# A fourth channel tile of the depthwise convolution on VectorE instead of TensorE

## The chip, the cores and the metric

The kernel runs on one core of a Trainium2 chip. The metric is the device time of one execution in microseconds. Five engines work side by side, each through its own fixed list of instructions: TensorE (PE; its weight loads are PEld), VectorE (DVE), ScalarE (ACT), GpSimd (POOL) and SyncE (SP). They wait for one another through semaphores. DMAs are issued from the queues of SP, POOL and ScalarE.

## The reference

One step of a two-layer streaming encoder, in float32, for two groups of requests: a prompt of 1024 frames and 8 running streams of 16 new frames each, 1152 rows in all, of width 1024. Layer 0 is differential attention beside a gated MLP. Layer 1, where the change lies, is a Conformer convolution module:

```python
xn = _rmsnorm(x, norm_g)
z = jnp.einsum('btd,de->bte', xn, w_in)
a, b, g = jnp.split(z, [C_WIDTH, 2 * C_WIDTH], axis=-1)
u = a * jax.nn.sigmoid(b)
...
c = lax.conv_general_dilated(ctx, w_dw[:, None, :], window_strides=(1,), padding='VALID',
                             feature_group_count=C_WIDTH) + b_dw
c = jax.nn.silu(_layernorm(c, ln_g, ln_b)) * jax.nn.silu(g)
y = x + jnp.einsum('btc,cd->btd', c, w_out)
```

`ctx` is `u` with 30 rows ahead of it: zeros for the prompt, the stored state for a running stream. The convolution is depthwise: each of the 1024 channels has its own 31 taps along time.

## The kernel before

Channels lie on partitions, 128 to a tile, so layer 1 has eight channel tiles, numbered 0 to 7. Each dense product is made of three float32r products (high by high, high by low, low by high; `mm3`, L157), whose weights are loaded, split into a high part on ScalarE (L145) and a low part on VectorE (L146). Weights are made one tile ahead.

`phase_conv` loops over the eight channel tiles and calls `conv_tile` (L1095) for each. It projects the 1152 rows in three chunks of 384 columns, first `b`, then `a`: six psum chunks of 24 products, from a pool `mm` of three psum buffers. ScalarE takes the sigmoid (L1133), VectorE multiplies `a` by it. Then there are two ways to do the 31 taps, and the constant `TAPS` says which tiles go the first way:

- Taps on VectorE. The product is written to a tile `u` (L1138), with the states put in by ScalarE (L1110) and the new frames by POOL (L1150). `taps()` multiplies `u`, shifted by k, with the k-th weight per channel and adds it to `cT`: for each k one instruction for the 8 streams (128 columns) and one for the prompt (1024 columns), L1171 for k = 0 and L1173 for the others. So a tile has 62 such instructions, and each depends on the one before it of the same width.
- Toeplitz products on TensorE. The product is written to `U` in another order (L1141), stored to DRAM (`s_u`, L1181) and loaded again as `X` (L1183), so that 8 time phases of a channel lie on neighbouring partitions. POOL builds the banded 32x32 weights `tw` (L1189). There are two steps, each of 80 products of 32x32x176 (`py`, L1198), which the trace lists as 160. ScalarE copies the result out (L1202), it goes through DRAM (`s_c`, L1208 to L1212) and VectorE adds the bias on the way back into `cT` (`back`, L1217 and L1220).

A tile's two Toeplitz steps are put into TensorE's list while the next tile is projected (`TOEP = (3, 4)`: behind the fourth and the fifth of its six chunks). For tile 7 they stand behind the first and second chunk of gate tile 1.

`back(i)` makes tile `i`'s taps, or its way back, and adds `cT[i]` to `msum` (L950, L952). It is called two tiles later: for a tile in `TAPS` after tile `i + 2` has been written down, for another inside tile `i + 2`. For tiles 6 and 7 it is called behind gate tiles 0 and 1. The order in which the program is written down gives each instruction a priority; a planner simulates the engines and fixes each engine's list by that.

After the eight tiles come eight gate tiles: three chunks each, from the same psum pool, with a silu on ScalarE (L980) into `sg`. Gate tiles 0 and 1 write into tiles that are also named `u`, and there are two buffers of that name for taps and gates together:

```python
u = self.up.tile([P, PAD + T + NB * 46], F32, name="u", bufs=2)
...
sg = [cp.tile([P, PAD + T + NB * 46], F32, name="u", bufs=2) for _ in range(2)]
```

The gates from 2 on (`sg`) lie in a pool that is opened where the convolution's work pool `ub` was, and so behind the last use of that, tile 7's way back. While the gate tiles are projected, the layernorm over channels runs in three column blocks (`norm_sum`, `norm_var`, `norm_apply`, L1005 to L1046), beginning behind the eleventh gate chunk. Last comes the output product, row tile by row tile.

Of the kernel before, what the change touches and what calls it, by code (L numbers as in the profile page):

```python
# [90 lines left out]
WL = ((0, 0, 2, 2), (2, 0, 2, 0))  # L91
VMID = False
TOEP = (3, 4)
TAPS = (0, 2, 4)
BACK = 3
HPT = 400
TAIL = 1
# [7 lines left out]
class Builder:  # L105
# [809 lines left out]
    def phase_conv(self):  # L915
        nc, tc, a = self.nc, self.tc, self.a
        with ExitStack() as st:
# [28 lines left out]
            def back(i):  # L946
                tiles[i][2]()
                done.append(cT[i])
                if len(done) == 2:
                    nc.vector.tensor_tensor(msum, done[0], done[1], ALU.add)  # L950
                elif len(done) > 2 and i < 7:
                    nc.vector.tensor_tensor(msum, msum, cT[i], ALU.add)  # L952

            def hooks_of(i):
                hooks = {}
                if i > 0:
                    hooks[TAIL] = [tiles[i - 1][0]]
                    for p, f in zip(TOEP, tiles[i - 1][1]):
                        hooks.setdefault(p, []).append(f)
                return hooks  # L960

            for i in range(8):
                wb = self.split_w(wp, [a["w_in1"][:, i * P:(i + 1) * P],
                                       a["w_in1"][:, D + i * P:D + (i + 1) * P]], 256)
                late = (lambda j=i - 2: back(j)) if i > 1 and i - 2 not in TAPS else None
                tiles.append(self.conv_tile(i, wb, pm, ub, cT[i], chan, wdw, (s_u, s_c), same, hooks_of(i), late))
                if i - 2 in TAPS:
                    back(i - 2)
# [126 lines left out]
    def conv_tile(self, i, wb, pm, ub, cv, chan, wdw, scr, same, hooks, late):  # L1095
# [8 lines left out]
        for n in range(2):  # L1104
            nc.tensor.transpose(ps[:, n * 120:(n + 1) * 120], sn[:120, n, :], self.ident[:120, :120])
        if i in TAPS:
            u = self.up.tile([P, PAD + T + NB * 46], F32, name="u", bufs=2)
# [20 lines left out]
        for c in range(3):  # L1128
# [7 lines left out]
            n = 384 if c < 2 else 256  # L1136
            if i in TAPS:
                mu = nc.vector.tensor_tensor(u[:, PAD + c * 384:PAD + c * 384 + n], pa_[:, :n], sb[:, :n], ALU.mult)  # L1138
# [7 lines left out]
            if c == 2:  # L1146
                nc.vector.tensor_tensor(utmp, pa_[:, 224:384], sb[:, 224:], ALU.mult)
                nw = utmp[:, 32:]
                if i in TAPS:
                    nc.gpsimd.tensor_copy(us[:, :, PAD:], nw.rearrange("p (b k) -> p b k", k=NQ))  # L1150
# [23 lines left out]

        if i in TAPS:
            return tail, (), taps
# [73 lines left out]
```

## Time and profile before

| | |
|---|---|
| median of 3 runs | 1223.09 us (1223.04 to 1224.46) |
| the profiled execution | 1223.68 us, span of its instructions 1221.9 us |
| granted TensorE clock, mean | 0.979 |
| TensorE busy | 1156.0 us |
| VectorE busy | 731.6 us |
| ScalarE busy | 456.8 us |
| POOL busy | 340.7 us |
| taps on VectorE (L1173) | 180 instructions, 779.4 to 959.4 us |
| Toeplitz products (L1198) | 1600 products in 10 steps, 829.5 to 1018.6 us |

All times inside an execution are in microseconds from the first instruction. A row of a timeline has start, duration, engine, line, operation, what is written and read, the shape, how many instructions are drawn together, and in brackets the idle time of the engine before it and what ended it. A row of a stage view has the stretch, its length, and for each engine the busy time and the number of instructions; then the granted clock, the busy share of the DMA engines, and GB/s.

### The profile page before, as it was taken

How to read it: one execution, taken by the hardware profiler on the slowest of the kernel's cores; microseconds unless marked ns; L12 is line 12 of the kernel's file. 1: busy time of each engine (PE TensorE's matmuls, PEld its weight loads, DVE VectorE, ACT ScalarE, POOL GpSimd, SP SyncE). 2: the span in 40 equal slices, each digit the busy share in tenths (PEclk: the TensorE clock that was granted, in tenths of full speed). 3: DMA queues.
4: the chain of work that ended last, by engine and by line, in shares of the span. 5: the costliest groups of instructions: out<-in, count | busy, mean ns of one | idle time of the engine just before them, and what ended most of it. 6: DMA issues, size and time to landing. Idle time of an engine off the chain costs nothing. (4 is left out here: it accounts for less than half of the span.)

```text
span 1221.9 us, 20908 instructions
## 1 busy us (share of the span) xinstructions
PE 1156.0 (95%) x7886; PEld 1024.1 (84%) x7886; DVE 731.6 (60%) x1560; ACT 456.8 (37%) x1065; POOL 340.7 (28%) x510
## 2 busy tenths in 40 slices
PE   6999999999989998679999999999999999998997
PEld 4878998899989997457777677899999899996886
DVE  4420225678788878766556444698999711377443
ACT  4431223445454545555444334312121222365221
POOL 2233223334434435413322231212131220350000
PEclk9999999999989998879999999999999999998999
DMA  8453435324132313867767635333332442113331
GB/s 302 110 169 91 144 118 172 107 71 121 46 89 78 108 50 105 301 214 242 258 226 255 192 125 190 92 91 96 93 96 90 140 134 84 35 35 104 104 104 69
DMA packets 125365, 160.33 MB, mean 131 GB/s; under 512 B 16514, under 2 KB 87194, under 8 KB 125257
## 3 DMA queue, kind: packets, MB, share of 16 engines
q1 hardware_dynamic: 109344, 106.95, 28.5%
q0 software_dynamic: 15776, 51.79, 12.9%
q8 instruction: 62, 1.02, 0.3%
q14 instruction: 39, 0.31, 0.1%
q10 hardware_dynamic: 144, 0.26, 0.1%
HBM read 119.41 MB, written 40.00 MB: 130 GB/s over the span
## 5 line engine op out<-in xcount | busy, mean ns | idle before, releaser
L157 PE MATMUL mm<-yh,wh 128*128 128x384 f32 x576 | 196.5, 341 | 3.3 <-ACT sb L1133 2.5
L157 PE MATMUL mm<-yl,wh 128*128 128x384 f32 x576 | 193.9, 337 | 0.5 <-issue 0.5
L157 PE MATMUL mm<-yh,wl 128*128 128x384 f32 x576 | 193.8, 338 | 0.3 <-DVE wl L146 0.2
L157 PE MATMUL mm<-wh,xh 128*128 128x384 f32 (+1 forms) x504 | 185.4, 369 | 2.5 <-DVE sg L468 1.4
L157 PE MATMUL mm<-wl,xh 128*128 128x384 f32 (+1 forms) x504 | 184.5, 366 | 0.9 <-DVE wl L146 0.9
L157 PE MATMUL mm<-wh,xl 128*128 128x384 f32 (+1 forms) x504 | 183.7, 364 | 0.0
L146 DVE TENSOR_TENSOR wl<-raw,wh 128x1024 fp32r<-128x1024 f32 (+1 forms) x72 | 84.3, 1178 | 104.7 <-ACT wh L145 102.7
L1173 DVE SCALAR_TENSOR_TENSOR cT<-u,cc,cT 128x128 f32<-128x128 f32 (+1 forms) x180 | 141.3, 843 | 1.0
L157 PEld LDWEIGHTS mm<-yh,wh 128*128 128x128 f32 x576 | 108.7, 189 | 6.2 <-issue 2.8
L157 PEld LDWEIGHTS mm<-yh,wl 128*128 128x128 f32 x576 | 108.6, 189 | 2.0 <-DVE wl L146 0.9
L157 PEld LDWEIGHTS mm<-yl,wh 128*128 128x128 f32 x576 | 108.7, 189 | 1.1 <-issue 0.7
L157 PEld LDWEIGHTS mm<-wh,xh 128*128 128x128 f32 x504 | 95.7, 190 | 13.3 <-DVE sg L468 1.4
L157 PEld LDWEIGHTS mm<-wl,xh 128*128 128x128 f32 x504 | 95.9, 190 | 10.5 <-DVE wl L146 1.8
L157 PEld LDWEIGHTS mm<-wh,xl 128*128 128x128 f32 x504 | 95.7, 190 | 8.7 <-DVE xl L170 0.3
L145 ACT CAST wh<-raw 128x1024 fp32r<-128x1024 f32 (+1 forms) x72 | 71.8, 1001 | 73.0 <-PE mm L157 30.9
L126 POOL TENSOR_TENSOR rr<-pw,mhalf 128x1 f32<-128x1 f32 x59 | 33.0, 559 | 200.3 <-DVE pw L125 190.8
L559 ACT ACTIVATE e<-S,nm 128x512 f32<-128x512 f32 (+5 forms) x96 | 55.1, 579 | 42.1 <-DVE nm L554 26.4
L157 PE MATMUL out<-wh,ch 128*128 128x512 f32 x144 | 59.9, 416 | 2.0 <-DVE xr L845 1.2
L157 PE MATMUL mm<-wh,ch 128*128 128x512 f32 x144 | 57.1, 397 | 4.5 <-ACT ch L1079 4.5
L551 DVE TENSOR_REDUCE nm<-S 128x1 f32<-128x512 f32 (+5 forms) x96 | 52.5, 551 | 12.6 <-PE S L546 11.9
L777 DVE TENSOR_TENSOR vl<-vraw,vh 128x1024 fp32r<-128x1024 f32 x32 | 43.2, 1351 | 26.8 <-ACT vh L776 26.6
L157 PE MATMUL out<-wh,cl 128*128 128x512 f32 x144 | 58.8, 408 | 0.0
(282 smaller groups left out, 2300.6 us busy)
## 6 DMA issues: line engine op xcount, KB each, us to landing
raw<-in_cache_k SPq DMA_DIRECT2D x32, 512.0 KB, 4.4
vraw<-in_cache_v POOLq DMA_DIRECT2D x32, 512.0 KB, 5.7
raw<-in_w_in SPq DMA_DIRECT2D x24, 512.0 KB, 5.3
raw<-in_w_out SPq DMA_DIRECT2D x16, 512.0 KB, 5.0
raw<-in_w_in SPq DMA_DIRECT2D x32, 256.0 KB, 4.0
raw<-in_w_in SPq DMA_DIRECT2D x48, 128.0 KB, 2.8
s_y<-xr POOLq DMA_DIRECT2D x9, 512.0 KB, 4.7
x<-s_y SPq DMA_DIRECT2D x9, 512.0 KB, 4.3
```

The source lines that it names most:

```text
L126: m = nc.gpsimd.tensor_tensor(out, v[:, :w], self.mhalf[:, :w], ALU.pow)
L145: nc.scalar.copy(h[:, :ks * n], raw[:, :ks * n])
L146: (low or nc.vector).tensor_tensor(l[:, :ks * n], raw[:, :ks * n], h[:, :ks * n].bitcast(F32), ALU.subtract)
L157: m = self.nc.tensor.matmul(out, lhsT=x, rhs=y, start=(i == 0), stop=(i == n - 1))
L551: nc.vector.tensor_reduce(nm[:, j:j + 1], s[:, :n], AX.X, ALU.max, negate=True)
L559: nc.scalar.activation(e[:, j * n:(j + 1) * n], S[j][:, :n], AF.Exp, bias=nv, accum_out=zz[:, j:j + 1])
L777: (nc.vector if i in VDVE else nc.gpsimd).tensor_tensor(vl, vr, vh.bitcast(F32), ALU.subtract)
L1173: nc.vector.scalar_tensor_tensor(dst, src, w1, dst, ALU.mult, ALU.add)
```

## The change

Channel tile 5 goes from the Toeplitz products to the taps; tiles 1, 3, 6 and 7 stay Toeplitz products. Nothing else is edited; what `conv_tile` and `back` do with tile 5 follows from the constant.

```diff
 VMID = False
 TOEP = (3, 4)
-TAPS = (0, 2, 4)
+TAPS = (0, 2, 4, 5)
 BACK = 3
 HPT = 400
```

## The prediction

> **What bounds the kernel now.** I read the busy shares and the chain first, then the conv layer by stage, then single engines' timelines.
>
> ```profile
> PE 1156.0 (95%) x7886; PEld 1024.1 (84%) x7886; DVE 731.6 (60%) x1560; ACT 456.8 (37%) x1065; POOL 340.7 (28%) x510
> ...
> PE 18%; DVE 1%; issue 1%; DMA 0%; ACT 0%; POOL 0%; DVEq 0%; POOLq 0%
> PE mm L157 16%; PE py L1198 1%; DMA big<-s_u 0%; DVE wl L146 0%; DVE cT L1044 0%; DVE cT L1064 0%; POOL nm L126 0%; PE ln L1009 0%; PE ln L1041 0%; PE ln L1010 0%; PE ln L1028 0%; PE ln L1029 0%; ACT wh L145 0%; DVE yo L195 0%; ACT yo L189 0%
> ```
>
> TensorE is busy 95% of the span and is nearly the whole of the last chain. The Toeplitz products (py, L1198) stand in that chain by themselves: what leaves TensorE shortens it, as long as no other engine becomes late. The stage view tells whether one does:
>
> ```profile
> core 0: us, PE busy (x) PEld busy (x) DVE busy (x) ACT busy (x) POOL busy (x), PEclk, DMA share, GB/s
> 871.00:902.00 31.00, 31.00 (x469) 29.31 (x468) 30.47 (x41) 5.96 (x17) 9.61 (x8) 1.00 0.38 110
> ...
> 927.00:959.00 32.00, 31.27 (x468) 29.19 (x467) 31.61 (x31) 5.92 (x17) 9.30 (x10) 1.00 0.36 110
> 959.00:992.00 33.00, 31.40 (x470) 29.71 (x469) 12.02 (x15) 6.30 (x17) 7.74 (x9) 1.00 0.42 125
> 1024.00:1109.00 85.00, 84.38 (x483) 81.35 (x481) 44.66 (x85) 39.25 (x74) 29.35 (x21) 1.00 0.17 54
> ...
> 961.00:1017.00 56.00, 53.88 (x793) 50.79 (x800) 14.60 (x19) 10.85 (x27) 11.59 (x14) 1.00 0.41 132
> ```
>
> The rows at 871, 927 and 959 are channel tiles 4, 6 and 7. While tile 6 is projected VectorE is full (31.61 of 32 us: the taps of tile 4); from 961 to 1017 it works only 14.60 of 56 us. The change puts a tile's taps into these 41.4 idle us.
>
> **What it takes off TensorE.** ScalarE's sigmoid of a tile's first chunk marks the pace of the tiles:
>
> ```profile
> 905.45 0.49 ACT L1133 ACTIVATE sb<-mm 128x384 f32<-128x384 f32 x1 [3.25 <-PE mm L157]
> 930.90 0.49 ACT L1133 ACTIVATE sb<-mm 128x384 f32<-128x384 f32 x1 [3.27 <-PE mm L157]
> 963.24 0.49 ACT L1133 ACTIVATE sb<-mm 128x384 f32<-128x384 f32 x1 [3.24 <-PE mm L157]
> 995.86 0.49 ACT L980 ACTIVATE u<-mm 128x384 f32<-128x384 f32 x1 [1.98 <-PE mm L157]
> ```
> ```profile
> 945.75 2.71 PE L1198 MATMUL py<-big,tw 32*32 32x176 f32 x160
> 950.67 2.62 PE L1198 MATMUL py<-big,tw 32*32 32x176 f32 x148
> 953.95 0.52 PE L1198 MATMUL py<-big,tw 32*32 32x176 f32 x12 [0.65 <-issue]
> ...
> 977.53 2.71 PE L1198 MATMUL py<-big,tw 32*32 32x176 f32 x160 [1.60 <-DMA big<-s_u]
> ```
>
> The rows are the first chunks of tiles 5, 6, 7 and of the gate. Tile 5, with no Toeplitz step inside, takes 930.90 - 905.45 = 25.45 us (six chunks of 4.24); tile 6, with both steps of tile 5 inside, 963.24 - 930.90 = 32.34 us. The difference, 6.9 us, is what tile 5's two steps cost: 2.71 and 3.28 us of products (with the 0.65 pause), and about 0.9 us around them. These 6.9 us come off. The Trainium skill, TensorEngine Tiling (Array Packing), Key Properties, says that a change of tiling mode drains TensorE; counting products alone the sum would be 6.0, and the 0.9 us more in the tile's pace agree with it.
>
> The next Toeplitz step, tile 6's first at 977.53, already waits 1.60 us for its input. That input begins with the multiplication of tile 6's last chunk on VectorE and goes through two DMAs on POOL's queue:
>
> ```profile
> 963.14 0.66 DVE L1141 TENSOR_TENSOR big<-mm,sb 128x256 f32<-128x256 f32 x1
> ...
> 965.66 0.59 POOL L1181 DMA_DIRECT2D s_u<-big  x1 [0.30 <-POOL big L1152]
> 972.34 0.92 POOL L1183 DMA_DIRECT2D big<-s_u  x1 [6.09 <-issue]
> ```
>
> From 963.14 to 977.53 are 14.4 us; TensorE has four chunks, 17.0 us, between the end of tile 6 and that step, so the multiplication may come 2.6 us after TensorE's end of the tile; now it comes 4.1 after (963.24 - 4.24 = 959.0). VectorE will now be full there. The wait lies between 0 (the DMAs meet no other traffic) and about 4 (6.6 us after); I take 3.3 for tile 6 and nothing for tile 7, so 1.7 more than now. TensorE's own balance: 6.9 - 1.7 = 5.2 us sooner.
>
> **What it puts on VectorE.**
>
> ```profile
> 805.00 7.36 DVE L1173 SCALAR_TENSOR_TENSOR cT<-u,cc,cT 128x1024 f32<-128x1024 f32 x10
> 947.81 12.88 DVE L1173 SCALAR_TENSOR_TENSOR cT<-u,cc,cT 128x1024 f32<-128x1024 f32 x8
> 960.73 1.36 DVE L952 TENSOR_TENSOR msum<-msum,cT 128x1152 f32<-128x1152 f32 x1
> 968.21 1.18 DVE L1217 TENSOR_SCALAR cT<-big,cc 128x1024 f32<-128x1024 f32 x1
> 969.32 0.45 DVE L1220 TENSOR_SCALAR cT<-big,cc 128x64 f32<-128x64 f32 x2
> 969.80 1.36 DVE L952 TENSOR_TENSOR msum<-msum,cT 128x1152 f32<-128x1152 f32 x1
> ```
> ```profile
> L1171 DVE TENSOR_SCALAR cT<-u,cc x6: 333/640/804, 778.6 to 905.7; 128x128 f32<-128x128 f32 x3, 128x1024 f32<-128x1024 f32 x3
> ...
> L1141 DVE TENSOR_TENSOR big<-mm,sb 128x384 f32<-128x384 f32 x10 | 9.1, 914 | 7.5 <-PE mm L157 5.1 <-issue 2.4
> L1138 DVE TENSOR_TENSOR u<-mm,sb 128x384 f32<-128x384 f32 x6 | 3.3, 555 | 1.9 <-ACT sb L1133 1.0 <-PE mm L157 0.9
> ```
>
> A pair of taps (1024 and 128 columns) takes 7.36 / 5 = 1.47 us, 30 pairs 44.1, and the first pair (L1171) 0.80 + 0.33: 45.2 us. Tile 4's taps end at 960.73; tile 5's three multiplications now write u (0.56 instead of 0.91), so 1.0 us sooner, 959.7. Tile 5's taps have their input from 933 on, but VectorE is full until then, so whether the two tiles' taps mix or follow one another, their sum ends at the same time. Other VectorE work that stays in the stretch is the 14.60 us less tile 5's way back (1.18 + 0.45) and its sum (1.36, which now comes after its taps): 11.6. Tile 5's taps end at 959.7 + 45.2 + 11.6 = 1016.5. Bounds: 1012.5 if the other work overlaps with neighbours as the pairs do, 1020 if a third of the multiplications wait on TensorE first.
>
> On POOL two builds of tw, one memset, two copies and two DMAs of tile 5 go, one memset (on u) and one copy come; on SP eight DMAs of the way back and the load of wx go; on ScalarE eight copies of 0.31. All of it lies beside TensorE's products, and I cost it at nothing. The memset of u waits for tile 2's taps (they end at about 903) with tw of tile 6 behind it on POOL; that is needed at 976, so this too is nothing.
>
> **Who waits for the taps.** The name "u" has two buffers, and the silus of gate tiles 0 and 1 are written into them next. Now gate tile 1 gets tile 4's, free at 960.7; afterwards it gets tile 5's, free at 1016.5.
>
> ```profile
> 1008.59 0.49 ACT L980 ACTIVATE u<-mm 128x384 f32<-128x384 f32 x1 [3.67 <-PE mm L157]
> 1010.92 0.93 ACT L1202 COPY big<-py 128x176 f32<-128x176 f32 x4 [1.84 <-PE py L1198]
> 1016.32 0.49 ACT L980 ACTIVATE u<-mm 128x384 f32<-128x384 f32 x1 [4.46 <-PE mm L157]
> 1018.60 0.95 ACT L1202 COPY big<-py 128x176 f32<-128x176 f32 x4 [1.79 <-PE py L1198]
> ...
> 1031.36 0.88 ACT L980 ACTIVATE sg<-mm 128x384 f32<-128x384 f32 x2 [6.74 <-DVE cT L1220]
> 1035.84 0.49 ACT L980 ACTIVATE sg<-mm 128x384 f32<-128x384 f32 x1 [3.60 <-PE mm L157]
> ```
>
> The first row is gate tile 1's first chunk. It will wait on ScalarE until 1016.5, and behind it stand, in the order of the rows, tile 7's copies out of its Toeplitz products, the second silu, and the last copies: 0.49 + 0.93 + 0.49 + 0.95 = 2.9 us, to 1019.4. From the last copies (now ending at 1019.55) tile 7's way back through DRAM to its add takes 11.8 us until gate tile 2's first silu (1031.36, released by that add; 0.45 us long): so this silu ends at 1019.4 + 11.8 + 0.45 = 1031.6. TensorE has three psum buffers and stops at gate tile 3 if the first silu of gate tile 2 isn't done. Gate tile 3 starts now at about 1035.8 (the row above is gate tile 2's last chunk). So TensorE can gain at most 1035.8 - 1031.6 = 4.2 us. The direct bound is wider: gate tile 2 starts three chunks before 1035.8, at 1023.1, and needs the first silu by then: with its 0.5 us, 1023.1 - 1017.0 = 6.1.
>
> The smaller of 5.2 and 4.2 counts: 4.2 us sooner at 1036. From 1024 to 1109 TensorE has 84.38 of 85 us, VectorE is half idle, and the chain after 1109 hangs on TensorE's last gate chunks, so the gain is kept to the end. Profiled execution 1223.68 us (its span 1221.9 and 1.8 around it) less 4.2 is 1219.5; the median of the runs is 0.6 lower, 1223.09, so 1218.9.
>
> **Rivals.**
> *More is gained.* If ScalarE's fixed order has tile 7's copies ahead of that silu, and the DMAs are faster so that the 1.60 us wait goes too: 6.9 + 1.6 = 8.5, time 1214.6. For it: the order is planned, and a planner that sees the late buffer would put the copies first. Against: the direct bound then needs taps that end by 1014.1.
>
> *The gain is eaten, no change.* The multiplications lag behind TensorE on the full VectorE: tile 6's last one starts at 963.14, 4.1 us after its products. Two more us of lag at both tiles make each Toeplitz input wait: 6.9 - 3.4 - 2 = 1.5 us, 1221.6. Against: from 871 to 902 VectorE is as full (30.47 of 31 us), and TensorE never stops.
>
> *POOL holds the taps.*
>
> ```profile
> 948.60 1.90 POOL L1189 TENSOR_TENSOR tw<-wx,same 128x640 f32<-128x640 f32 x1 [6.09 <-PE py L1198]
> ...
> L1189 POOL TENSOR_TENSOR tw<-wx,same 128x640 f32<-128x640 f32 x2 | 3.1, 1556 | 10.8 <-PE py L1198 10.8
> L1152 POOL COPY big<-utmp 128x128 f32<-128x128 f32 x2 | 1.8, 895 | 10.7 <-DVE utmp L1147 10.7
> ```
>
> Eight taps from 947.81 take 12.88 us where 8 x 1.32 is 10.6: they run beside builds of tw. Two builds leave tile 4's taps with tile 5's steps and two meet tile 5's taps now, which evens out in my sum. If each POOL operation held VectorE for its whole time, 3.1 + 1.8 = 4.9 us would come on top of 1016.5: taps end at 1021.4, TensorE loses 0.7, 1223.8. The Trainium skill, GPSIMD Engine Reference, Specifications, has GpSimd's SBUF interface shared with VectorE, with contention for VectorE instructions with two SBUF inputs, and the taps are such; the trace agrees for tw, and no row shows how far a copy holds them.
>
> *Slower.* VectorE doesn't find the holes. Its order is fixed beforehand, and a multiplication placed too early makes the taps behind it wait for TensorE. The stretch has 41.4 idle us and 3.0 that tile 5's way back and sum leave; the taps need all of it. The point that decides is the end of the taps: at 1020.7 nothing is gained (1035.8 less 15.1), after 1023.2 it is slower by over 0.2%. If 10 us of holes remain, they end at 1026.5 and TensorE stops 5.8 us: 1228.9. Against: in the full rows above, with taps at hand, it lost half a us each.
>
> **How the numbers follow.** Forecast (1217 to 1220.6) 0.46; more gained 0.12; eaten 0.14; POOL 0.08; slower 0.20. 0.2% is 2.4 us, about what can be told from no change: faster is 0.46 + 0.12 = 0.58, same 0.14 + 0.08 = 0.22, slower 0.20. The range goes from 1214.6 to 1226 (the slower case at taps ending near 1023.6); over it lies about half of the slower case, under it little.
>
> **What would show it.** Right: py x1280 instead of 1600; tile 6's pace near 25.5 us; VectorE full until about 1016; the taps' last row at 1012 to 1020; ScalarE's silu of gate tile 1 waiting on DVE L1173; TensorE stopping about a us near gate tiles 2 and 3. Wrong: TensorE waiting for multiplications (L1138, L1141) or for the weights' low parts (L146), which come after the taps in the program; taps ending after 1021; a longer wait than 4 us before a Toeplitz step.

## The result, and the profile after

The changed kernel takes 1233.95 us (median of 4 runs, 1231.08 to 1236.01) against 1223.32 us before (median of 4 runs, 1223.04 to 1224.46): ratio 1.0081, 95% interval 1.0064 to 1.0098. It is 10.6 us slower; 1218.9 was predicted, and the range ended at 1226.0. The profiled execution took 1234.51 us, its span 1232.7.

The busy shares, from the page of the changed kernel:

```profile
PE 1149.7 (93%) x7566; PEld 1020.4 (83%) x7566; DVE 774.0 (63%) x1619; ACT 454.1 (37%) x1057; POOL 337.9 (27%) x504
```

TensorE has 320 instructions and 6.3 us less, as the change says, but its share of the span fell, from 95% to 93%. Where it stopped, the list of TensorE's waits between 770 and 1130 us tells (total, times, longest):

```profile
PE trb L1158 <- DVE utmp L1147: 12.4, 1, 12.4
...
PE py L1198 <- DMA big<-s_u: 2.7, 2, 2.4
```

Before, that list has no wait of half a microsecond or more for a multiplication. Two stages (start and end, length, busy time by engine, then granted clock, DMA share, GB/s); the first is tile 6, now without a Toeplitz step inside:

```profile
927.00:953.00 26.00, 26.00 (x153) 25.91 (x152) 26.00 (x38) 4.79 (x9) 6.25 (x5) 1.00 0.16 49
...
961.00:1017.00 56.00, 41.26 (x505) 38.95 (x504) 55.65 (x57) 8.56 (x20) 12.57 (x14) 0.85 0.32 100
```

From 961 to 1017, where VectorE had 14.60 of 56 us, it now has 55.65; it left no holes. TensorE had 53.88 there and now has 41.26, at a clock of 0.85. So VectorE took a tile's worth of taps more into that stretch, as forecast, and the loss comes from the order in which it worked. VectorE's list there, row by row:

```profile
974.15 0.89 DVE L1141 TENSOR_TENSOR big<-mm,sb 128x384 f32<-128x384 f32 x1
974.86 19.82 DVE L1173 SCALAR_TENSOR_TENSOR cT<-u,cc,cT 128x1024 f32<-128x1024 f32 x19
994.61 1.35 DVE L952 TENSOR_TENSOR msum<-msum,cT 128x1152 f32<-128x1152 f32 x1
995.87 9.20 DVE L1173 SCALAR_TENSOR_TENSOR cT<-u,cc,cT 128x1024 f32<-128x1024 f32 x7
1004.99 1.22 DVE L146 TENSOR_TENSOR wl<-raw,wh 128x1024 fp32r<-128x1024 f32 x1
1006.12 1.28 DVE L1173 SCALAR_TENSOR_TENSOR cT<-u,cc,cT 128x1024 f32<-128x1024 f32 x1
1007.32 0.64 DVE L1141 TENSOR_TENSOR big<-mm,sb 128x256 f32<-128x256 f32 x1
1007.78 0.33 DVE L1147 TENSOR_TENSOR utmp<-mm,sb 128x160 f32<-128x160 f32 x1
...
1010.63 5.24 DVE L1173 SCALAR_TENSOR_TENSOR cT<-u,cc,cT 128x1024 f32<-128x1024 f32 x4
1015.90 2.75 DVE L952 TENSOR_TENSOR msum<-msum,cT 128x1152 f32<-128x1152 f32 x2
```

The first row is tile 7's second multiplication, the two at 1007 are its third and last. Between them stand 33 us of taps, a sum and a weight split, and TensorE waits for none of these there. And on TensorE:

```profile
972.12 3.93 PE L1198 MATMUL py<-big,tw 32*32 32x176 f32 x160 [2.39 <-DMA big<-s_u]
...
980.38 2.72 PE L1198 MATMUL py<-big,tw 32*32 32x176 f32 x160
...
1008.16 0.47 PE L1158 MATMUL trb<-cst,utmp 128*128 128x128 f32 x1 [12.36 <-DVE utmp L1147]
...
1009.29 0.52 PE L157 MATMUL mm<-yh,wl 128*128 128x384 f32 x1
...
1013.51 0.34 PE L157 MATMUL mm<-yl,wh 128*128 128x384 f32 x1
```

The transposes of tile 7's last columns (L1158) need that multiplication and stand behind the second chunk of gate tile 0. TensorE came to them at 1008.16 - 12.36 = 995.80; two chunks of 4.24 earlier, at about 987.3, tile 7's products were done. VectorE multiplied them 20 us later. The last two rows show that a product of one and the same shape took 0.52 us after the stop and 0.34 from 1013.5 on: the granted clock was halved. Two stretches carry that:

```profile
970.00:977.00 7.00, 4.88 (x166) 4.10 (x167) 7.00 (x9) 0.94 (x4) 0.73 (x2) 0.76 0.21 71
999.50:1013.20 13.70, 5.04 (x17) 4.97 (x18) 13.52 (x15) 0.41 (x2) 1.90 (x2) 0.50 0.29 97
```

The account, with times counted from the convolution's first sigmoid (771.94 before, 772.30 after), so that nothing ahead of it enters: the end comes 10.4 us later. Tile 7 starts 6.6 us sooner. The step at 972.12 waits 0.8 longer (2.39 for 1.60), and at the lower clock of its stretch (0.76) it takes 3.93 us for 2.71, so 1.2 more. The stop costs 12.4, and the 5.04 us of work at half clock behind it 2.5. Together -6.6 + 0.8 + 1.2 + 12.4 + 2.5 = +10.3.

ScalarE's rows show the pace and who else waited:

```profile
931.59 0.49 ACT L1133 ACTIVATE sb<-mm 128x384 f32<-128x384 f32 x1 [3.25 <-PE mm L157]
...
957.04 0.49 ACT L1133 ACTIVATE sb<-mm 128x384 f32<-128x384 f32 x1 [3.27 <-PE mm L157]
...
993.30 1.28 ACT L980 ACT_TABLE_LOAD   x1 [4.90 <-DVE cT L1173]
...
1019.33 0.49 ACT L980 ACTIVATE u<-mm 128x384 f32<-128x384 f32 x1 [3.72 <-PE mm L157]
```

The first two rows are the first chunks of tiles 6 and 7. At 993.30 the silu of gate tile 0 has waited until tile 4's taps ended: these ended at 960.73 before. The row at 1019.33 is gate tile 1's first silu: it waited for TensorE, not for its buffer, which the taps had left at 1015.9.

### The profile page after: what moved, and what is told of

Same layout as the page of the kernel before. It is cut to its first block, busy times and chain, and to the rows that moved or that the text cites. A ratio compares the mean times of both kernels' runs of the same rounds, so it can differ in the third digit from the quotient of the medians.

```text
span 1232.7 us, 20289 instructions
## 1 busy us (share of the span) xinstructions
PE 1149.7 (93%) x7566; PEld 1020.4 (83%) x7566; DVE 774.0 (63%) x1619; ACT 454.1 (37%) x1057; POOL 337.9 (27%) x504
## 4 chain that ended last, share of the span: by engine, by line
PE 74%; DVE 8%; DMA 8%; issue 5%; ACT 3%; POOL 1%; SPq 1%; DVEq 0%; POOLq 0%; ACTq 0%
PE mm L157 52%; PE out L157 7%; DMA vraw<-in_cache_v 2%; PE pa L588 2%; DVE cT L1173 2%; PE py L1198 2%; PE tr L167 1%; PE tr L417 1%; PE S L545 1%; PE S L546 1%; DMA raw<-in_w_out 1%; PE tr L583 1%; DVE wl L146 1%; DMA raw<-in_w_in 1%; DMA big<-s_u 1%
## 5 line engine op out<-in xcount | busy, mean ns | idle before, releaser
L1173 DVE SCALAR_TENSOR_TENSOR cT<-u,cc,cT 128x128 f32<-128x128 f32 (+1 forms) x240 | 184.7, 832 | 0.9
L551 DVE TENSOR_REDUCE nm<-S 128x1 f32<-128x512 f32 (+5 forms) x96 | 52.6, 552 | 12.9 <-PE S L546 12.1
```

The source lines that it names most:

```text
L551: nc.vector.tensor_reduce(nm[:, j:j + 1], s[:, :n], AX.X, ALU.max, negate=True)
L1173: nc.vector.scalar_tensor_tensor(dst, src, w1, dst, ALU.mult, ALU.add)
```

## The experiments

The theory: the loss is the place of one instruction, tile 7's last multiplication behind 33 us of taps in VectorE's fixed order. Its first rival is the bound of the prediction, gate tile 1's silu waiting for the buffer `u` of tile 5's taps. A second is that VectorE simply has too much to do, in whatever order. The table has all runs. Each ratio is to runs of the kernel before made beside that experiment, and these went from 1217.95 to 1230.87 us; hence the medians and intervals. `rank` and `tail5` were run once. The other columns are read from the profiled execution of each kernel. Three are starts, counted from its first sigmoid of the convolution: tile 7's last multiplication, gate tile 1's first silu, and the second sigmoid of the convolution. The last is the time from that second sigmoid to the end.

| | median us | ratio to before, 95% | tile 7's last multiplication | gate tile 1's first silu | second sigmoid | from there to the end |
|---|---|---|---|---|---|---|
| before | 1223.32 |  | 220.3 | 236.7 | 11.0 | 439.0 |
| after | 1233.95 | 1.0081 [1.0064, 1.0098] | 235.5 | 247.0 | 11.0 | 449.4 |
| hold12 | 1225.85 | 1.0004 [0.9981, 1.0026] | 212.8 | 249.3 | 11.0 | 441.0 |
| toeplate | 1226.59 | 1.0005 [0.9986, 1.0023] | 209.0 | 240.6 | 9.4 | 439.4 |
| taps6 | 1229.33 | 1.0031 [1.0013, 1.0048] | 221.7 | 245.9 | 11.0 | 444.8 |
| notaps5 | 1216.38 | 0.9916 [0.9887, 0.9946] | 210.2 | 226.6 | 9.4 | 430.6 |
| own | 1233.84 | 1.0067 [1.0044, 1.0091] | 235.3 | 247.0 | 11.0 | 448.9 |
| hold12half | 1216.13 | 0.9916 [0.9891, 0.9941] | 212.4 | 228.9 | 11.0 | 431.6 |
| own_before | 1225.54 | 0.9997 [0.9978, 1.0015] | 220.8 | 237.2 | 11.0 | 438.4 |
| own_late | 1217.79 | 0.9930 [0.9910, 0.9949] | 210.5 | 231.7 | 11.0 | 434.1 |
| rank | 1233.98 | one run | 233.3 | 244.5 | 9.5 | 450.1 |
| tail5 | 1232.97 | one run | 235.1 | 246.6 | 11.0 | 449.1 |
| own_taps6 | 1221.58 | 0.9965 [0.9949, 0.9981] | 222.5 | 232.4 | 12.1 | 438.1 |

Ends are compared from the second sigmoid on, because the stretch between the two sigmoids differs although no edit bears on it. TensorE waits 2.53 us for the first one in all thirteen; here are that wait and the second sigmoid in `before` and in `notaps5`:

```profile
772.48 0.45 PE L157 MATMUL mm<-yh,wh 128*128 128x384 f32 x1 [2.53 <-ACT sb L1133]
782.93 0.49 ACT L1133 ACTIVATE sb<-mm 128x384 f32<-128x384 f32 x1 [4.33 <-PE mm L157]
```
```profile
774.97 0.44 PE L157 MATMUL mm<-yh,wh 128*128 128x384 f32 x1 [2.53 <-ACT sb L1133]
783.86 0.49 ACT L1133 ACTIVATE sb<-mm 128x384 f32<-128x384 f32 x1 [4.36 <-PE mm L157]
```

Behind the wait the granted clock was 0.50 from 774 to 777 in `before`, and 1.00 throughout in `notaps5`, `toeplate` and `rank`. That alone is 1.6 us. `own_taps6` was at half clock for longer, which gives its 12.1.

**The place alone.** `hold12` lets tile 5's taps from k = 12 on follow tile 7's last multiplication:

```diff
+    mt = nc.vector.tensor_tensor(utmp, pa_[:, 224:384], sb[:, 224:], ALU.mult)
+    self.mt = mt.ins if hasattr(mt, "ins") else mt
...
+    with ExitStack() as held:
+        if i == 5 and k >= 12:
+            held.enter_context(tc.issue_after(self.mt))
```

> The changed kernel with one edge more: tile 5's taps from k = 12 on stand in VectorE's list behind tile 7's last multiplication (L1147). No work is added or taken. Theory (place): TensorE's stop of 12.4 us before the transposes of utmp, and the half clock after it (about 2.4 us), come from the place of that multiplication behind 27 taps of tile 5; then both go, and the time is 1217 to 1221, 13 to 17 us below the changed kernel's 1234. Rival (amount): VectorE simply has more work than the stretch holds, or the silus of gate tile 1 wait for the taps; then the multiplication is early but TensorE stops elsewhere, and the time stays at 1228 or more.

The multiplication comes 22.7 us sooner, the stop at the transposes is gone, and the end comes 8.4 us sooner than after the change. That is most of the 10.4, yet 1217 to 1221 was missed. What is left stands in TensorE's waits and in the rows of ScalarE and VectorE of this run:

```profile
PE mm L157 <- ACT u L980: 6.6, 1, 6.6
```
```profile
997.69 0.49 ACT L980 ACTIVATE u<-mm 128x384 f32<-128x384 f32 x1 [3.62 <-PE mm L157]
1021.99 0.87 ACT L980 ACTIVATE u<-mm 128x384 f32<-128x384 f32 x2 [16.87 <-DVE cT L1177]
1022.75 0.94 ACT L1206 COPY big<-py 128x176 f32<-128x176 f32 x4
```
```profile
992.95 1.20 DVE L1221 TENSOR_SCALAR cT<-big,cc 128x1024 f32<-128x1024 f32 x1 [5.68 <-DMA big<-s_c]
```

With the first wait away the second one ends last: ScalarE stands 16.87 us in front of gate tile 1's silu until the taps free the buffer, tile 7's last copies (L1206) behind it. This is the prediction's bound, in its place. Part of that wait is the edit's own doing: VectorE's new order has tile 6's way back (L1221) ahead of most of the held taps, VectorE stands still 5.68 us for it, and the taps end at 1021.9 instead of 1015.9.

**The same place by another way.** `toeplate` leaves VectorE's order to the planner and puts tile 6's two Toeplitz steps behind tile 7's last chunk instead of inside it:

```diff
-                    for p, f in zip(TOEP, tiles[i - 1][1]):
+                    for p, f in zip((5, 5) if i == 7 else TOEP, tiles[i - 1][1]):
```

> The changed kernel with both Toeplitz steps of tile 6 behind tile 7's last projection chunk instead of inside the tile; taps untouched. Theory (place, and why): the planner holds a Toeplitz step for much longer than the 2.7 us it takes and therefore places tile 7's last multiplication far down; with no step ahead of that chunk it is placed in time by itself, TensorE's stop at the transposes is under 2 us, and the time is 1217 to 1224. Rival (amount): the taps themselves push the multiplication back; then it stays behind them and the time is within 3 us of the changed kernel's 1234.

The multiplication comes in time by itself (209.0), and the stop at the transposes is gone. The end comes 10.0 us sooner than after the change and 0.4 us later than before; the ratio can't be told from 1, and 1217 to 1224 was missed. The waits, POOL's rows and ScalarE's row of gate tile 1's first silu:

```profile
PE py L1198 <- DMA big<-s_u: 7.0, 1, 7.0
```
```profile
983.20 14.44 POOL L1152 COPY big<-utmp 128x128 f32<-128x128 f32 x1 [7.56 <-DVE utmp L1147]
997.93 0.58 POOL L1181 DMA_DIRECT2D s_u<-big  x1 [0.30 <-POOL big L1152]
998.54 4.07 POOL L1189 TENSOR_TENSOR tw<-wx,same 128x640 f32<-128x640 f32 x2
1002.55 0.95 POOL L1183 DMA_DIRECT2D big<-s_u  x1
```
```profile
1014.37 0.50 ACT L980 ACTIVATE u<-mm 128x384 f32<-128x384 f32 x1 [17.14 <-DVE cT L1173]
```

Now POOL's copy of the new frames takes 14.44 us beside the taps, the store follows it, the load of `X` follows that, and TensorE waits 7.0 us for tile 7's step. ScalarE waits for the buffer here too, 17.14 us, but TensorE's list shows no wait for that silu.

**Another tile.** `taps6` has tile 6 in the place of tile 5, so the new taps start after the multiplications that matter:

```diff
-TAPS = (0, 2, 4, 5)
+TAPS = (0, 2, 4, 6)
```

> Tile 6 instead of tile 5 is the fourth tile of taps (tiles 1, 3, 5, 7 Toeplitz). The same TensorE work goes (two steps), the same 62 tap instructions come, but the taps of 4 and 6 follow one another and tile 7 has no Toeplitz step inside. Theory (place): tile 7's last multiplication is in time, TensorE gains 6.9 us of steps and the 1.6 us wait of tile 6, less what the silus of gate tile 1 wait for u: 1215 to 1221. Rival (amount): any fourth tile costs VectorE's 45 us too much; 1228 or more.

The median, 1229.33, falls where the rival put it (1228 or more) and not where the theory did (1215 to 1221), and the end comes 5.8 us later than before. Yet TensorE doesn't stop for half a us at the transposes. The wait is the buffer's, one step on:

```profile
PE py L1198 <- ACT big L1202: 6.5, 1, 6.5
```
```profile
1013.64 0.49 ACT L980 ACTIVATE u<-mm 128x384 f32<-128x384 f32 x1 [8.34 <-DVE cT L1173]
```

ScalarE waited 8.3 us for the taps before gate tile 1's silu, and the copies out of the Toeplitz products stood behind it.

**What TensorE's side is worth.** `notaps5` leaves out taps 1 to 30 of tile 5, so its output isn't the reference's:

```diff
-            for k in range(CONV):
+            for k in range(1 if i == 5 else CONV):
```

> The changed kernel with tile 5's taps k = 1 to 30 left out (its convolution is then wrong): TensorE's side of the change alone. Both theories: the two steps' 6.9 us and up to 1.6 us of a wait go and nothing comes, 1214.5 to 1217.5. If it is 1220 or more, the steps taken off TensorE are worth less than their pace showed.

The end comes 8.4 us sooner than before, and the time is in the range. That is the 6.9 + 1.6 that I had at most: the two steps go, and so does the wait at tile 6's step.

**The buffer alone.** `own` writes gate tile 1 into a tile of its own, and gate tile 2 into the buffer `u` in its place; the space comes from one buffer less of `big`:

```diff
-            sg = [cp.tile([P, PAD + T + NB * 46], F32, name="u", bufs=2) for _ in range(2)]
+            sg = [cp.tile([P, PAD + T + NB * 46], F32, name="u", bufs=2), cp.tile([P, TOK], F32, name="sg1"),
+                  cp.tile([P, PAD + T + NB * 46], F32, name="u", bufs=2)]
...
-            U = ub.tile([P, 8, 180], F32, name="big", bufs=4)
+            U = ub.tile([P, 8, 180], F32, name="big", bufs=3)
...
```

> The changed kernel with gate tile 1's silu in a tile of its own (gate tile 2 takes the second buffer of u instead; the convolution's big tiles go from four buffers to three to make room). VectorE's list as in the changed kernel. Theory (two stops in a row, the place of the multiplication first): TensorE still stops about 12 us before the transposes of utmp, and the time stays within 3 us of the changed kernel, 10 us above the kernel before. Rival (the buffer of u alone): with the buffer free the loss goes, and the time is within 3 us of the kernel before or below it.

```profile
PE trb L1159 <- DVE utmp L1148: 12.3, 1, 12.3
```

The stop of the changed kernel is there unchanged, and so is the time. The rival doesn't explain the result; it is second in line.

**Half the taps.** `hold12half` is `hold12` without taps 15 to 30 of tile 5 (output not the reference's):

```diff
-            for k in range(CONV):
+            for k in range(15 if i == 5 else CONV):
```

> As hold12, with tile 5's taps k = 15 to 30 left out (its convolution is then wrong), so that the multiplication is in time and the taps end some 22 us earlier. Theory (in hold12 the whole remaining loss is gate tile 1's silu waiting for the end of the taps): TensorE no longer waits for that silu, and the end lies 8 to 10 us before that of the kernel before, measured from the convolution's first sigmoid, as with notaps5. Rival (a full VectorE slows TensorE by many small waits): no more than 5 us.

The end comes 7.4 us sooner than before, a little less than the 8 to 10 expected, with no stop for taps or silu. So the amount of taps matters too, by way of the buffer: with 16 pairs of 1.47 us less, 24 us, the silu is on time.

**Both waits.** `own_before` is the control, the kernel before with the tiles of `own`; `own_late` is the change with the edits of `own` and `toeplate` together, all taps in it:

```diff
-                    for p, f in zip(TOEP, tiles[i - 1][1]):
+                    for p, f in zip((5, 5) if i == 7 else TOEP, tiles[i - 1][1]):
...
+            sg = [cp.tile([P, PAD + T + NB * 46], F32, name="u", bufs=2), cp.tile([P, TOK], F32, name="sg1"),
...
```

> Control: the kernel before with the same tiles for the gates and three big buffers instead of four, taps of tiles 0, 2, 4 only. Both theories: nothing waits for these, so within 2 us of the kernel before. If it is faster or slower, the memory alone counts in the other runs.

> Both stops taken away: tile 6's Toeplitz steps behind tile 7's last chunk, and gate tile 1's silu in a tile of its own. All 62 taps of tile 5 are there. Theory: TensorE keeps what it gained, 6 to 10 us before the kernel before, measured from the convolution's first sigmoid, and the ratio is 0.992 to 0.996. Rival (amount): VectorE's 45 us find another place to show, and the time is within 2 us of the kernel before.

The control doesn't move (0.9997). `own_late` is faster than both kernels, 0.7% under the one before, and its end comes 4.9 us sooner, less than the 6 to 10 expected. Its waits, VectorE's row of the multiplication, POOL's copy behind it, and its stages:

```profile
PE mm L157 <- ACT u L980: 1.8, 1, 1.8
```
```profile
979.80 0.33 DVE L1148 TENSOR_TENSOR utmp<-mm,sb 128x160 f32<-128x160 f32 x1
```
```profile
980.20 1.42 POOL L1153 COPY big<-utmp 128x128 f32<-128x128 f32 x1 [13.40 <-DVE utmp L1148]
```
```profile
843.00:985.00 142.00, 142.00 (x1401) 138.42 (x1400) 141.45 (x190) 24.81 (x56) 31.75 (x33) 1.00 0.30 92
985.00:1012.00 27.00, 25.20 (x424) 23.21 (x423) 26.61 (x24) 5.71 (x16) 3.79 (x4) 0.94 0.36 110
```

Over 142 us TensorE has no idle time and VectorE half a microsecond. So a full VectorE by itself doesn't stop TensorE, and the second rival falls. What remains against `notaps5` is 3.5 us: the wait of 1.8 for gate tile 0's silu, which hangs on tile 4's late taps, and about 1.6 by the clock (27 us at 0.94). Against `toeplate` not only the buffer is different: POOL's copy takes 1.42 us here and 14.44 there, which the edit doesn't account for, so the 5.3 us between the two can't be put to the buffer alone.

**Is it the priority?** `rank` raises the priority of `conv_tile`'s multiplications far above that of the taps (L1138, L1141 and L1147; the edit is shown for one):

```diff
-                mu = nc.vector.tensor_tensor(dst, pa_[:, :n].rearrange("p (m f) -> p m f", f=8),
-                                             sb[:, :n].rearrange("p (m f) -> p m f", f=8), ALU.mult)
+                with tc.high_priority(offset=4000):
+                    mu = nc.vector.tensor_tensor(dst, pa_[:, :n].rearrange("p (m f) -> p m f", f=8),
+                                                 sb[:, :n].rearrange("p (m f) -> p m f", f=8), ALU.mult)
```

> The changed kernel with all of conv_tile's multiplications (L1138, L1141, L1147) raised 4000 places in the planner's rank. Theory (in the plan tile 7's last product isn't finished yet when VectorE looks for work): rank changes nothing, the multiplication stays behind 27 taps of tile 5, TensorE stops 12 us, 1230 to 1236. Rival (it is ready, but ranks behind tile 4's taps): it comes before them, the stop is under 3 us, and the time is 1220 to 1228.

```profile
PE trb L1161 <- DVE utmp L1150: 9.2, 1, 9.2
PE py L1201 <- DMA big<-s_u: 5.8, 2, 5.0
```

The multiplication stays behind the taps (233.3) and TensorE still stops there, 9.2 us instead of the 12 expected, so low priority isn't why it is there. `toeplate` moved it by moving Toeplitz steps. The reading that fits both is that the planner takes the product for unfinished, because it gives the steps ahead of it more time than their 2.72 us; no run shows the planner's times, and this stays open.

**Is it the transposes?** `tail5` gives them four chunks more, behind the sixth chunk of the next tile instead of the second:

```diff
-TAIL = 1
+TAIL = 5
```

> The changed kernel with the transposes of utmp (the tail) four chunks later, behind the sixth chunk instead of the second. Theory (the late multiplication also holds a psum buffer): TensorE runs one or two products further and then stops for a psum buffer instead, 8 to 12 us, time 1228 to 1235. Rival (only the transposes were in the way): no stop over 3 us and 1225 or less.

```profile
1006.60 0.66 PE L157 MATMUL mm<-yh,wh 128*128 128x384 f32 x1 [15.01 <-DVE utmp L1147]
```

The stop moves to the projection and grows, beyond the 8 to 12 us expected: the product that isn't multiplied holds one of three psum buffers. More slack for one reader doesn't help; the multiplication itself is what is late.

**Tile 6 with its own buffer.** `own_taps6` is `own` with tile 6 for tile 5:

```diff
-TAPS = (0, 2, 4, 5)
+TAPS = (0, 2, 4, 6)
...
+            sg = [cp.tile([P, PAD + T + NB * 46], F32, name="u", bufs=2), cp.tile([P, TOK], F32, name="sg1"),
...
```

> Tile 6 instead of tile 5 as the fourth tile of taps, and gate tile 1's silu in a tile of its own. Theory: in taps6 the loss was that silu waiting for the taps (8.3 us on ScalarE) and tile 7's copies behind it (TensorE 6.5 us); both go, and the end is 3 to 8 us before that of the kernel before, measured from the convolution's first sigmoid, ratio 0.993 to 0.998. Rival: the loss of taps6 lay in VectorE's amount of work; within 2 us of taps6 (5.8 us behind the kernel before).

It is faster than before (0.9965, in the range), less so than `own_late`. In the profiled execution, 1228.67 us and the longest of its twelve, the end comes 0.9 us sooner, so 3 to 8 us was missed there. Its waits and POOL's row:

```profile
PE py L1199 <- DMA big<-s_u: 5.2, 2, 3.6
```
```profile
999.65 5.48 POOL L1153 COPY big<-utmp 128x128 f32<-128x128 f32 x1 [22.29 <-DVE utmp L1148]
```

The copy ahead of tile 7's `X` is slow beside the taps, as in `toeplate`.

## Why the prediction was wrong, step by step

*Products off TensorE, 6.9 us.* Right: tile 6's pace is 957.04 - 931.59 = 25.45 us, tile 7 starts 6.6 us sooner, and `notaps5`, where the wait of 1.6 goes too, ends 8.4 sooner. One reading under it was short: tile 5's second step lasts from 950.67 to 953.95 + 0.52, so 3.80 us with the pause and not 3.28, and 0.4 us are left around the two steps instead of 0.9. The 6.9 comes from the pace and doesn't rest on this; the agreement seen in the 0.9 does.

*Tile 6's input, 3.3 us of wait for 1.60.* The wait is 2.39, within the bounds. That the products behind it run at a lower clock (3.93 us for 2.71) was not in the sum.

*VectorE's sum.* Right: forecast 1016.5 as the taps' end, and the last ones end at 1010.63 + 5.24 = 1015.9. There are no holes, so the rival "Slower" with its 10 us of holes didn't happen: slower came by another road.

*"Whether the two tiles' taps mix or follow one another, their sum ends at the same time."* True of the sum and wrong as a reason to stop there. They did mix: tile 4's taps, ended at 960.73 before, now end just before 993.30, and gate tile 0's silu waited for that. In `own_late` this is still the 1.8 us of TensorE.

*The lag of the multiplications.* This is the step that failed: "I take 3.3 for tile 6 and nothing for tile 7". I worked out a lag for tile 6 from its rows and gave tile 7 none, though its multiplications stand in the stretch that my own sum had filled to the last microsecond. Its lag was 20 us (987.3 to 1007.3), and it made most of the loss: `hold12` and `toeplate`, two different ways of putting the multiplication right, take back 8.4 and 10.0 of the 10.4 us. A gain they don't bring; other waits stand behind this one. The rival "eaten" named this mechanism and gave it 2 us, and "Slower" looked at the opposite order, a multiplication placed too early with taps behind it. What I argued from, that full stages before showed no stop, was an observation of an order that the change itself made anew.

*Gate tile 1's buffer, a gain of at most 4.2 us.* The mechanism is right (`hold12`, `taps6`), but hidden behind the other in the changed kernel. `hold12` also checks its size: there the silu starts at 249.3 against 236.7, and the end is 2.0 us later than before. The prediction's sum, by which nothing is gained at 1020.7 (248.8 counted from the first sigmoid), makes that about 0.5 later; it didn't have the half clock behind the wait (0.50 from 1022 to 1026).

*POOL beside the taps.* The rival had POOL hold VectorE, and the taps ended on time all the same (1015.9). What cost TensorE time in `toeplate` and `own_taps6` goes the other way: POOL's copy is slow while VectorE is full.

## What to carry to other kernels

When an idle engine is filled, the question isn't only when its work ends but where in its list the short instructions stand that others wait for: look for the last psum eviction of each tile, and give it a lag of as much as the filler that can stand in front of it. A fixed order made by a planner is made anew by any change of load, so rows of before tell durations better than positions. And a wait that ends last hides the next: here the misplaced multiplication, the shared buffer and the late copy on POOL came up one after the other, and with all of tile 5's taps in the kernel only `own_late`, where none of the three is left, brought a gain.

## What the runs showed of the chip

*A POOL copy can take many times as long beside a full VectorE.* The copy `big<-utmp` of 128x128 takes 0.44 us where no taps run beside it (tile 7 in `notaps5`), 0.50 to 2.56 in most places beside them, and 5.48 to 14.44 in four, two of them shown above (`toeplate`, `own_taps6`). The DMA that needs it was issued 0.3 us after its end, so these are no mere roughness of the record. In `own_late` it takes 1.42 us beside the same sequence of VectorE instructions as in `toeplate`; what decides between the two, no run shows.

```profile
984.99 0.44 POOL L1152 COPY big<-utmp 128x128 f32<-128x128 f32 x1 [3.62 <-DVE utmp L1147]
```

The Trainium skill, GPSIMD Engine Reference, Specifications, names contention between the two for VectorE instructions with two SBUF inputs, and the taps are such; these rows agree and show that POOL's side of it can be thirty times the 0.44 us.

*A short stop can be followed by half the clock, and need not be.* After the wait of 2.39 us the step's stretch had a clock of 0.76, and in `own_late` half the clock follows a wait of only 1.80 us:

```profile
995.00 0.44 PE L157 MATMUL mm<-yh,wh 128*128 128x384 f32 x1 [1.80 <-ACT u L980]
...
996.91 0.52 PE L157 MATMUL mm<-yh,wh 128*128 128x384 f32 x1
```

Products of 0.33 to 0.35 us take 0.52 there. The wait of 1.60 us in the kernel before was followed by a step of 2.71 us, at full clock, and so was one of 1.78 us in `taps6`:

```profile
1002.64 2.71 PE L1198 MATMUL py<-big,tw 32*32 32x176 f32 x160 [1.78 <-DMA big<-s_u]
```

The wait of 2.53 us for the convolution's first sigmoid, the same in all thirteen kernels, was followed by half the clock in ten profiled executions and by full clock in three. So the length of the stop alone doesn't decide, and that alone makes executions differ by 1.6 us. The Trainium skill, TensorE: Matmul & The Clock Gate, What's actually happening, gives an idle window of about 3.4 us, free-running, as what halves the clock; here half the clock also followed waits of 1.80 to 2.53 us, and the two outcomes of one and the same wait fit a window that doesn't begin with it.
